# State space stage of a 512-token, three-block kernel: the turn before the norm's factor, tables by tile in HBM, fixed state buffers

## The chip, the cores and the metric

The kernel runs on one core of a Trainium2 chip. The metric is the device time of one execution in microseconds; before the change the median of 3 runs is 2787.21 us (2784.18 to 2787.91). Everything is in single precision. A product of two matrices is made of three matmuls: each operand is split into a high part (`Xh`, `whi`) and a low part (`Xl`, `wlo`), and high×high, low×high and high×low are added up.

## The reference, cut to what matters

512 tokens of 1024 channels pass through two layers and then a second block. The change touches the state space mixer of the second layer and the group norm of the retention in the second block:

```python
h = rms_norm(x, norm_mix[1])
y = s5_mixer(h, ...)                 # 64 groups of 16 channels, 64 complex states each
g_a, g_b = split(gelu(y) @ od_w_glu, 2)
x = x + g_a * sigmoid(g_b)

# s5_mixer: u -> B u -> x_t = a x_(t-1) + (B u)_t -> Re(C x) + d u
bu_re = einsum('gpc,bsgc->bsgp', bb_re, uf)      # and bu_im
_, _, xr, xi = associative_scan(combine, (a_r, a_i, bu_re, bu_im), axis=1)
y = einsum('gcp,bsgp->bsgc', c_re, xr) - einsum('gcp,bsgp->bsgc', c_im, xi) + d * uf

# retention, per head: r is 512 tokens x 256
r = (r - mean(r)) * rsqrt(var(r) + 1e-5) * gn_g
```

`rms_norm` multiplies each token by one factor, 1 / sqrt(mean of squares + eps), and each channel by its gain.

## The kernel before

The activations lie transposed: eight tiles `x[m]` of 128 channels by 512 tokens. All work is written in order per engine and the engines are ordered by semaphores; each engine runs its own instructions in program order, DMA issues included (SP issues most loads, ACT issues some DMAs). Weights come in tiles of 1 MB (`fetch`), and `cook` splits each into `whi` (ACT) and `wlo` (DVE or POOL, L342) one tile ahead of its use.

**Tables.** For the state space mixer, tables are made from its parameters while the first layer's feed-forward part runs (`s5_tables`, called step by step as `side` of `conv_ffn(0, ...)`): 16 steps, two for each tile of 128 channels; each step writes one block of 960 KB to HBM (`tabs[it]`, L1138). A block holds G (input into the turned states), C (states to output) and E (the rotations that turn the complex recurrence into a real one).

**The stage.** After the PLE part of layer one (`ple(0, ...)`, which adds up the squares of `x` tile by tile in `Rms.add`) the factor of the norm is made: sums over channels by matmul (L204), root on ACT (L177), three small DVE operations (L179 to L182), a diagonal matrix (`diag`, L190), a matmul that spreads it over the partitions (L197) and a copy `st_r` (L198). Then there are eight units, one for each tile of `x`. Per unit: `drive` makes `h` = x × gain × factor on DVE with the tokens taken in four phases (L1226) and writes it to HBM (`hd`, L1228); `lift` reads it back as `up`, with phases and channels turned into the partition axis (L1234); `load` reads the three tables (L1221). `mid` feeds: 16 matmuls of `up` with G (L1241), then six rotations with E on DVE (L1244 to L1249); `scan` runs the recurrence (two scans on DVE, L1260) and rotates back with E on POOL (L1267 to L1273; `xr` of odd units on DVE) into `xr` and `xi`, whose column zero is the state before the first token; `emit` makes 24 matmuls with C (L1281), GELU on ACT (`g`), a DMA out and `y` back (L1288); `land` splits `y` into `Gh` and `Gl`, which feed the GLU matmuls. A unit is fed at step t, scanned at t + 1, emitted at t + 2, landed at t + 3. The first half of the first GLU tile (`acc0[1]`) is multiplied between the units, the second half (`acc0[0]`) behind them.

**The retention.** `Head.retain` multiplies scores and values per head, takes mean and variance per token (BN_STATS and BN_AGGR on DVE), copies the variances to `gnv` (L1610), makes the factor with `rstd_of` (L174 to L182) and writes `rn` (L1613). `turn` transposes `rn` on PE (L1620) and scales it. The depthwise convolution's taps (L1519, DVE) are issued between the parts of a head, eight or sixteen at a time (`taps`).

## Time and profile before

| | us |
|---|---|
| median of 3 runs | 2787.21 |
| the profiled execution | 2786.97 |
| its span, first to last instruction | 2785.2 |
| TensorE (PE) busy | 2698.1 |
| VectorE (DVE) busy | 1581.5 |
| ScalarE (ACT) busy | 992.5 |
| GpSimd (POOL) busy | 666.9 |

The span leaves out what lies before the first and behind the last instruction, 1.8 us. Engines run beside each other, so their busy times overlap. The mean granted clock of TensorE is 0.987 of its full speed.

### The profile page before, as it was taken

What the parts mean: (1) busy time and instruction counts of PE and PEld (TensorE: products, weight loads), DVE (VectorE), ACT (ScalarE), POOL (GpSimd) and SP (SyncE); (2) the same over time, 40 slices, a digit from 0 to 9 for tenths busy, and PEclk for the clock granted to TensorE, in tenths of its full rate; (3) what the DMA queues carried; (4) which work ended last, traced back from release to release, by engine and by line L of the source; (5) the groups of instructions that cost most, each with busy time, mean ns of one, the idle gap of its engine ahead of it and who ended that gap; (6) DMA issues with size and microseconds to landing.
All of it is one profiled execution on the core that took longest, in us unless ns stands there. A gap on an engine that the chain in (4) does not pass through costs nothing. (4 is left out here: it accounts for less than half of the span.)

```text
span 2785.2 us, 35089 instructions
## 1 busy us (share of the span) xinstructions
PE 2698.1 (97%) x14355; PEld 2275.0 (82%) x14355; DVE 1581.5 (57%) x2478; ACT 992.5 (36%) x1295; POOL 666.9 (24%) x590
## 2 busy tenths in 40 slices
PE   8999999999579999999999999999999999999998
PEld 8978888887468888888888888887888788989888
DVE  5456968686654656466333335866387764733335
ACT  5544424344213423244212125333333352432222
POOL 2213035762351000002000026354443421300000
PEclk9999999999789999999999999999999999999999
DMA  5203334433762223224322232322222223222222
GB/s 162 76 31 107 99 105 148 148 132 133 224 207 91 91 91 101 96 76 136 101 96 91 92 105 82 95 82 81 97 81 97 76 91 109 89 91 91 91 95 72
DMA packets 277840, 289.80 MB, mean 104 GB/s; under 512 B 20197, under 2 KB 266951, under 8 KB 277680
## 3 DMA queue, kind: packets, MB, share of 16 engines
q1 hardware_dynamic: 256208, 260.38, 28.8%
q10 hardware_dynamic: 20640, 26.78, 2.7%
q8 instruction: 112, 1.84, 0.3%
q0 software_dynamic: 832, 0.41, 0.1%
q14 instruction: 48, 0.39, 0.0%
HBM read 263.43 MB, written 24.12 MB: 103 GB/s over the span
## 5 line engine op out<-in xcount | busy, mean ns | idle before, releaser
L339 ACT CAST whi<-raw 128x2048 fp32r<-128x2048 f32 (+2 forms) x216 | 406.3, 1881 | 761.4 <-PE ps L366 600.4
L365 PE MATMUL ps<-Xh,whi 128*128 128x512 f32 (+1 forms) x1472 | 567.4, 387 | 0.4 <-ACT Xh L302 0.4
L342 DVE TENSOR_TENSOR wlo<-raw,whi 128x2048 fp32r<-128x2048 f32 (+2 forms) x167 | 381.0, 2282 | 325.9 <-ACT whi L339 324.5
L366 PE MATMUL ps<-Xl,whi 128*128 128x512 f32 (+1 forms) x1472 | 563.0, 383 | 0.6 <-POOL Xl L305 0.6
L367 PE MATMUL ps<-Xh,wlo 128*128 128x512 f32 (+1 forms) x1472 | 562.7, 383 | 0.8 <-DVE wlo L342 0.8
L342 POOL TENSOR_TENSOR wlo<-raw,whi 128x2048 fp32r<-128x2048 f32 (+1 forms) x49 | 223.5, 4561 | 688.1 <-ACT whi L339 362.9
L365 PEld LDWEIGHTS ps<-Xh,whi 128*128 128x128 f32 x1472 | 276.2, 188 | 58.9 <-issue 3.2
L367 PEld LDWEIGHTS ps<-Xh,wlo 128*128 128x128 f32 x1472 | 276.7, 188 | 58.2 <-DVE wlo L342 1.6
L366 PEld LDWEIGHTS ps<-Xl,whi 128*128 128x128 f32 x1472 | 277.1, 188 | 56.9 <-issue 1.2
L365 PE MATMUL ps<-XBh,whi 128*128 128x512 f32 (+1 forms) x736 | 281.9, 385 | 1.0 <-ACT whi L339 1.0
L366 PE MATMUL ps<-XBl,whi 128*128 128x512 f32 (+1 forms) x736 | 281.0, 383 | 0.5 <-POOL XBl L305 0.5
L367 PE MATMUL ps<-XBh,wlo 128*128 128x512 f32 (+1 forms) x736 | 281.4, 384 | 0.0
L366 PE MATMUL ps<-Al,whi 128*128 128x512 f32 (+1 forms) x528 | 202.1, 383 | 1.5 <-DVE Al L305 1.5
L365 PE MATMUL ps<-Ah,whi 128*128 128x512 f32 (+1 forms) x528 | 202.6, 386 | 0.0
L367 PE MATMUL ps<-Ah,wlo 128*128 128x512 f32 (+1 forms) x528 | 202.5, 384 | 0.0
L1519 DVE SCALAR_TENSOR_TENSOR ps<-glu,par,ps 128x512 f32<-128x512 f32 x232 | 174.1, 751 | 4.1
L366 PEld LDWEIGHTS ps<-XBl,whi 128*128 128x128 f32 x736 | 138.2, 188 | 30.3 <-POOL XBl L305 0.9
L367 PEld LDWEIGHTS ps<-XBh,wlo 128*128 128x128 f32 x736 | 138.1, 188 | 29.9
L365 PEld LDWEIGHTS ps<-XBh,whi 128*128 128x128 f32 x736 | 137.6, 188 | 29.3 <-ACT whi L339 1.4
L222 POOL TENSOR_TENSOR st_a<-st_a,st_q 128x512 f32<-128x512 f32 x25 | 44.3, 1770 | 489.4 <-ACT st_q L220 489.3
L374 PE MATMUL ps<-whi,Xh 128*128 128x256 f32 (+1 forms) x512 | 147.6, 289 | 0.7 <-ACT z L608 0.4
L375 PE MATMUL ps<-wlo,Xh 128*128 128x256 f32 (+1 forms) x512 | 144.7, 283 | 0.0
(482 smaller groups left out, 4826.2 us busy)
## 6 DMA issues: line engine op xcount, KB each, us to landing
raw<-in_ffn_w_up_dram SPq DMA_DIRECT2D x66, 1024.0 KB, 5.1
raw<-in_w_in_dram SPq DMA_DIRECT2D x40, 1024.0 KB, 5.1
raw<-in_ffn_w_down_dram SPq DMA_DIRECT2D x32, 1024.0 KB, 4.8
raw<-in_ffn_w_gate_dram SPq DMA_DIRECT2D x22, 1024.0 KB, 5.2
tab<-tabs ACTq DMA_DIRECT2D x16, 960.0 KB, 3.9
raw<-in_ffn_w_down_dram SPq DMA_DIRECT2D x16, 768.0 KB, 4.1
raw<-in_ev_w_in_dram SPq DMA_DIRECT2D x8, 1024.0 KB, 5.2
raw<-in_ple_w_gate_dram SPq DMA_DIRECT2D x8, 1024.0 KB, 4.9
```

The source lines that it names most:

```text
L222: eng.tensor_tensor(self.acc, self.acc, sq, op=ALU.add)
L339: cp = act.copy(hi, rv)
L342: lo.tensor_tensor(lw, rv, hi.bitcast(F32), op=ALU.subtract)
L365: pe.matmul(acc, wh[j][:, s], X.h[k], start=start and t == 0, stop=False)
L366: pe.matmul(acc, wh[j][:, s], X.l[k], start=False, stop=False)
L367: pe.matmul(acc, wl[j][:, s], X.h[k], start=False, stop=stop and t == len(ks) - 1)
L374: pe.matmul(acc, X.h[k][:, s], wh[j], start=start and t == 0, stop=False)
L375: pe.matmul(acc, X.h[k][:, s], wl[j], start=False, stop=False)
L1519: vec.scalar_tensor_tensor(x[m] if t == 30 else acc, u[:, t:t + T], col("ck", t * KD + m), acc, op0=ALU.mult, op1=ALU.add)
```

## The change

- **Tables by tile.** A table block of HBM now holds one kind of table of one unit (4 phases), in rows of 4 KB or 6.5 KB: 48 DMAs write them instead of 16, and a unit loads with 3 DMAs on ACT's queue instead of 6 on SP's. Those of the first units are loaded during the PLE part.
- **Early turn.** `turn_in` makes `h` = x × gain on ACT, without the factor, as soon as PLE has done a tile, and `hd` and `up` follow at once.
- **The factor in turned order.** `rr` (each token's factor at its phase, 128 × 128, DVE) goes through one matmul with `l4` (L1345), which gives the factor in the order of the turned input; a copy `rbt`, and `norm` multiplies `up` by it: unit 0 on DVE, units 1 to 7 on POOL (L1250). `diag`, the spread matmuls and `st_r` go.
- **Fixed buffers.** Two pairs `xr`, `xi` and two `rm`, whose column zero is set once by six memsets. Back rotations of unit 7 run on DVE, the real part of units 0, 2, 4, 6 on POOL and of the odd ones on DVE.
- **Order of PE.** A unit is fed one step ahead; six eighths of `acc0[0]` are multiplied between the last units.
- **Elsewhere.** `Rms` uses two buffers for squares; a `warm` root on ACT is written ahead of tile 7's turn; POOL's weight split is cut into four operations; `retain` takes the variances without the copy, and the taps that followed or filled it are held behind the last `rn`.

```diff
--- before.py
+++ after.py
@@ cook @@
-            lo.tensor_tensor(lw, rv, hi.bitcast(F32), op=ALU.subtract)
+            q = kt * n // 4 if lo is pool else kt * n
+            for o in range(0, kt * n, q):
+                lo.tensor_tensor(lw[:, o:o + q], rv[:, o:o + q], hi[:, o:o + q].bitcast(F32), op=ALU.subtract)
@@ s5_tables @@
-            nc.scalar.dma_start(tabs[it], tab.rearrange("p q n -> p (q n)"))
+            i = it % 2
+            for z, (lo, hi) in CUT.items():
+                nc.scalar.dma_start(tabs[it // 2][z][:, 2 * i:2 * i + 2, :], tab[:, :, lo:hi])
@@ Unit @@
+            def table(self, tag, bufs):
+                lo, hi = CUT[tag]
+                t = ep.tile([P, 4, hi - lo], F32, tag=tag, name=nm(tag), bufs=bufs)
+                nc.scalar.dma_start(t, tabs[self.k][tag])
+                return t
...
+            def turn_in(self):
                 k = self.k
...
+                h = ep.tile([P, 4, P], F32, tag="h", name=nm("h"), bufs=2)
+                act.activation(h, x[k].rearrange("p (n j) -> p j n", j=4), AF.Copy, scale=col("norm_mix", KD + k))
+                nc.scalar.dma_start(hdr[k], h)
+                self.up = ep.tile([P, 4, P], F32, tag=f"Gh{k}", name=nm("up"))
+                src = hdr[k].rearrange("(i c) j n -> j c i n", c=32)
                 for b in range(4):
                     nc.sync.dma_start(self.up[32 * b:32 * b + 32], src[3 - b])
+            def norm(self, eng):
+                eng.tensor_tensor(self.up, self.up, rbt.unsqueeze(1).to_broadcast([P, 4, P]), op=ALU.mult)
@@ around ple @@
+        def ready(m):
+            rms2.add(m)
+            if m == KD - 1:
+                warm = sm.tile([P, 1], F32, tag="warm", name="warm")
+                act.activation(warm, eps_r, AF.Sqrt)
+            units[m].turn_in()
...
+        def phases():
+            b = bank((P, P))
+            pe.matmul(b, l4, rms2.rr.rearrange("p i n -> p (i n)"), start=True, stop=True)
+            vec.tensor_copy(rbt, b)
...
+        units[0].norm(vec)
+        units[0].feed()
+        units[2].load_g()
+        for k in range(1, KD):
+            units[k].norm(pool)
@@ the loop over units @@
+            if at(t + 1):
+                at(t + 1).feed()
+            if at(t + 3):
+                at(t + 3).load_g()
+            if at(t):
+                at(t).spin()
+                if at(t - 1) and t % 2 == 0:
+                    at(t - 1).real(vec)
...
+            if t == KD:
+                acc0[0] = [bank() for _ in range(2)]
+                mm_fm(acc0[1], w0s[1], G, [4], start=False, stop=False, js=[4])
+                for k in range(3):
+                    mm_fm(acc0[0], w0s[0], G, [k], start=k == 0, stop=False, js=[k])
@@ retain @@
-                vv = sm.tile([P, NT], F32, tag="gn_v", name=nm("gnv"))
-                vec.tensor_copy(vv, mv[:, :, 1])
-                r = rstd_of(vv, NT, LN_EPS)
+                r = rstd_of(mv[:, :, 1], NT, LN_EPS)
@@ the loop over heads @@
-                hd_.retain()
-                taps(8)
-            taps(16)
+                with tc.issue_after(hd_.retain().ins):
+                    taps(8 if j == 0 else 24)
```

Three places show how the change moves instructions. The first is DVE at the end of the PLE part, where the norm's factor (`rr`) is made; `st_a` holds the sum of squares. Before (six more rows L1226 follow, then the first rotation):

```order
L222 TENSOR_TENSOR st_a_6024<-st_a_6024,st_q_6447 128x512
L174 TENSOR_SCALAR ps_6516<-ps_6516 128x4
L179 RECIPROCAL rr_6523<-ps_6516 128x4
L180 SCALAR_TENSOR_TENSOR ps_6516<-ps_6516,rr_6523 128x4
L181 TENSOR_TENSOR ps_6516<-ps_6516,rr_6523 128x4
L182 SCALAR_TENSOR_TENSOR rr_6523<-ps_6516,rr_6523 128x4
L190 TENSOR_TENSOR diag_6528<-cst,rr_6523 128x512
L1226 SCALAR_TENSOR_TENSOR h_6567<-x_72,par,st_r_6550 128x512
L1226 SCALAR_TENSOR_TENSOR h_6570<-x_73,par,st_r_6550 128x512
```

After:

```order
L225 TENSOR_TENSOR st_a_6091<-st_a_6091,sq_6592 128x512
L174 TENSOR_SCALAR ps_6671<-ps_6671 128x4
L179 RECIPROCAL rr_6678<-ps_6671 128x4
L180 SCALAR_TENSOR_TENSOR ps_6671<-ps_6671,rr_6678 128x4
L181 TENSOR_TENSOR ps_6671<-ps_6671,rr_6678 128x4
L182 SCALAR_TENSOR_TENSOR rr_6678<-ps_6671,rr_6678 128x4
L1339 TENSOR_TENSOR rr<-s_6093,rr_6678 128x128
L1346 COPY rbt<-ps_6705 128x128
L1250 TENSOR_TENSOR up_6348<-up_6348,rbt 128x512
L1265 TENSOR_TENSOR s_896_6764<-tE_6371,ps_6725 128x512
L1266 TENSOR_TENSOR ps_6725<-tE_6371,ps_6725 128x512
```

The eight products `h` and the diagonal are gone from between the factor and the first rotation of unit 0 (the row that writes `s` from `tE` and `ps`, L1244, now L1265); a factor of 128 columns, a copy and one product take their place.

The second place is ACT ahead of the root of that factor (L177): squares of the last two tiles (`st_q`, `sq`), copies and DMAs of the PLE part (`Xl`, `pjd`). Before:

```order
L220 ACTIVATE st_q_6439<-x_78 128x512
L913 DMA pjd<-Xh_848_6476 128x512
L913 DMA pjd<-Xh_849_6477 128x512
L220 ACTIVATE st_q_6447<-x_79 128x512
L908 COPY Xl_852_6496<-ps_6498 128x512
L908 COPY Xl_853_6497<-ps_6499 128x512
L913 DMA pjd<-Xl_852_6496 128x512
L913 DMA pjd<-Xl_853_6497 128x512
L177 ACT_TABLE_LOAD
L177 ACTIVATE ps_6516<-ps_6516 128x4
```

After:

```order
L223 ACTIVATE sq_6592<-x_79 128x512
L1243 DMA hd_2561<-h_6579 128x512
L1242 ACTIVATE h_6597<-x_79,par 128x512
L921 DMA pjd<-Xh_870_6631 128x512
L1243 DMA hd_2562<-h_6597 128x512
L921 DMA pjd<-Xh_871_6632 128x512
L916 COPY Xl_874_6651<-ps_6653 128x512
L916 COPY Xl_875_6652<-ps_6654 128x512
L921 DMA pjd<-Xl_874_6651 128x512
L921 DMA pjd<-Xl_875_6652 128x512
L177 ACT_TABLE_LOAD
L177 ACTIVATE ps_6671<-ps_6671 128x4
```

The turned tiles `h` with their DMAs (L1242, L1243) now stand between the squares and the root, and the table load still stands just ahead of it.

The third place is DVE in the fourth retention head, from the variances (`mv`) to `rn`; L1519 (L1604 after) is a tap of the convolution. Before:

```order
L1610 COPY gnv_14708<-mv_14663 128x4
L1519 SCALAR_TENSOR_TENSOR ps_14654<-glu_14138,par,ps_14654 128x512
L174 TENSOR_SCALAR rv_14710<-gnv_14708 128x4
L1519 SCALAR_TENSOR_TENSOR ps_14654<-glu_14138,par,ps_14654 128x512 x3
L179 RECIPROCAL rr_14714<-rt_14712 128x4
L1519 SCALAR_TENSOR_TENSOR ps_14654<-glu_14138,par,ps_14654 128x512
L180 SCALAR_TENSOR_TENSOR rt_14712<-rv_14710,rr_14714 128x4
L1519 SCALAR_TENSOR_TENSOR ps_14654<-glu_14138,par,ps_14654 128x512
L181 TENSOR_TENSOR rt_14712<-rt_14712,rr_14714 128x4
L1519 SCALAR_TENSOR_TENSOR ps_14654<-glu_14138,par,ps_14654 128x512
L182 SCALAR_TENSOR_TENSOR rr_14714<-rt_14712,rr_14714 128x4
L1519 SCALAR_TENSOR_TENSOR ps_14654<-glu_14138,par,ps_14654 128x512
```

After:

```order
L1692 BN_AGGR mv_14738<-bs_14777 128x2
L1692 BN_AGGR mv_14738<-bs_14780 128x2
L174 TENSOR_SCALAR rv_14783<-mv_14738 128x4
L179 RECIPROCAL rr_14787<-rt_14785 128x4
L180 SCALAR_TENSOR_TENSOR rt_14785<-rv_14783,rr_14787 128x4
L181 TENSOR_TENSOR rt_14785<-rt_14785,rr_14787 128x4
L182 SCALAR_TENSOR_TENSOR rr_14787<-rt_14785,rr_14787 128x4
L1696 TENSOR_SCALAR rn_14737<-ps_14739,mv_14738,rr_14787 128x256 x2
L1696 TENSOR_SCALAR rn_14737<-ps_14755,mv_14738,rr_14787 128x256 x2
L1604 SCALAR_TENSOR_TENSOR ps_14729<-glu_14203,par,ps_14729 128x512 x4
L1706 SCALAR_TENSOR_TENSOR gnt_14872<-ps_14867,par,sg_14725 128x512
L1604 SCALAR_TENSOR_TENSOR ps_14729<-glu_14203,par,ps_14729 128x512
```

The copy `gnv` and eight taps that stood among the small operations are gone from there; `rn` follows the factor at once, and the taps come behind it.

## Rows read from the trace of the kernel before

**Rows 1.** The page: span, and busy time of each engine
```profile
span 2785.2 us, 35089 instructions
...
PE 2698.1 (97%) x14355; PEld 2275.0 (82%) x14355; DVE 1581.5 (57%) x2478; ACT 992.5 (36%) x1295; POOL 666.9 (24%) x590
```

**Rows 2.** Windows of the state space stage: PE, PEld, DVE, ACT, POOL busy (instructions), TensorE clock, DMA share, GB/s
```profile
720.00:740.00 20.00, 5.80 (x25) 5.56 (x26) 9.66 (x12) 0.00 (x0) 0.00 (x0) 0.50 0.87 285
740.00:800.00 60.00, 36.45 (x225) 33.88 (x224) 44.01 (x57) 11.53 (x16) 43.54 (x46) 0.71 0.74 221
...
840.00:860.00 20.00, 20.00 (x88) 16.23 (x87) 9.23 (x7) 5.63 (x8) 1.88 (x1) 1.00 0.34 106
700.00:840.00 140.00, 89.77 (x482) 77.01 (x481) 84.07 (x106) 32.80 (x48) 60.58 (x66) 0.78 0.68 210
```

**Rows 3.** Waits of PE from 700 to 840: total us, times, longest
```profile
PE ps L1241 <- DMA up<-hd: 19.5, 2, 13.4
PE ps L1241 <- DMA tG<-tab: 12.7, 3, 10.9
PE ps L365 <- ACT Gh L302: 10.6, 3, 6.0
```

**Rows 4.** Timeline of ACT from 708: start, duration, line, operation
```profile
708.40 0.63 ACT L220 ACTIVATE st_q<-x 128x512 f32<-128x512 f32 x1 [0.76 <-DVE st_a L222]
...
710.42 1.28 ACT L177 ACT_TABLE_LOAD   x1 [0.43 <-ACT Xl L908]
711.71 0.16 ACT L177 ACTIVATE ps<-ps 128x4 f32<-128x4 f32 x1
```

**Rows 5.** Timeline of DVE from 712 to 742
```profile
712.72 0.69 DVE L190 TENSOR_TENSOR diag<-cst,rr 128x512 f32<-128x512 f32 x1
...
736.99 0.68 DVE L1244 TENSOR_TENSOR s<-tE,ps 128x512 f32<-128x512 f32 x1
...
740.58 1.21 DVE L1260 TENSOR_TENSOR_SCAN zi<-s,ps 128x512 f32<-128x512 f32 x1
```

**Rows 6.** Timeline of PE, the last matmul of the last unit
```profile
824.76 0.39 PE L1281 MATMUL ps<-xi,tC 128*128 128x128 f32 x2
```

**Rows 7.** Timeline of POOL around 767
```profile
766.55 1.27 POOL L1269 TENSOR_TENSOR xr<-s,s 128x512 f32<-128x512 f32 x1
767.78 1.27 POOL L1273 TENSOR_TENSOR xi<-v,v 128x512 f32<-128x512 f32 x1
```

**Rows 8.** Timeline of DVE around 755
```profile
755.10 1.74 DVE L1269 TENSOR_TENSOR xr<-s,s 128x512 f32<-128x512 f32 x1 [2.72 <-POOL s L1267]
```

**Rows 9.** Timeline of ACT from 824
```profile
835.16 0.62 ACT L302 CAST Gh<-y 128x512 fp32r<-128x512 f32 x1 [8.23 <-DMA y<-hd]
```

**Rows 10.** Waits of PE from 1400 to the end
```profile
PE ps L1620 <- DVE rn L1613: 8.4, 4, 3.4
```

**Rows 11.** Timeline of DVE in one retention head
```profile
1905.62 0.17 DVE L1607 BATCH_NORM_AGGREGATE mv<-bs 128x2 f32<-128x6 f32 x1
...
1906.41 2.73 DVE L1610 COPY gnv<-mv 128x4 f32<-128x4 f32 x1
...
1915.24 1.90 DVE L1613 TENSOR_SCALAR rn<-ps,mv,rr 128x256 f32<-128x256 f32 x4
```

**Rows 12.** Timeline of POOL in the same head
```profile
1904.51 4.61 POOL L342 TENSOR_TENSOR wlo<-raw,whi 128x2048 fp32r<-128x2048 f32 x1 [6.61 <-ACT whi L339]
```

**Rows 13.** Timeline of PE in the same head
```profile
1915.93 0.41 PE L1620 MATMUL ps<-cst,rn 128*128 128x128 f32 x2 [3.35 <-DVE rn L1613]
```

**Rows 14.** Window around the other long wait of this kind, columns as in rows 2
```profile
2160.00:2180.00 20.00, 16.65 (x69) 13.51 (x68) 16.90 (x30) 2.37 (x4) 6.89 (x3) 0.83 0.16 53
```

**Rows 15.** DMA queues from 760 to 826: packets, MB, share of the window
```profile
q1 hardware_dynamic: 12564, 12.46, 63.8%
```

**Rows 16.** DMA queues from 380 to 640
```profile
q10 hardware_dynamic: 2160, 14.75, 13.7%
```

**Rows 17.** Window of the stage in which the tables are made
```profile
380.00:640.00 260.00, 257.74 (x1576) 207.67 (x1575) 199.19 (x357) 102.50 (x151) 155.93 (x242) 1.00 0.39 138
```

More of the change, by code (lines that the diff above doesn't have):

```diff
@@ L218, in add @@
             else:
-                sq = stile("st_q")
+                if self.two and self.n % 2:
+                    sq = xp.tile([P, T], F32, tag="diag", name=nm("sq"), bufs=2)
+                else:
+                    sq = stile("st_q")
                 act.activation(sq, x[m], AF.Square)
@@ L1199, in tile_net @@
             pass
-    rms2 = Rms()
-    rb2 = ple(0, X, rms, rms2.add, (rms2.fin1, rms2.fin2))
-    with tc.tile_pool(name="s5r", bufs=1) as rp:
+    with tc.tile_pool(name="s5e", bufs=1) as ep, ExitStack() as late:
+        rms2 = Rms(two=True)
         G = Act([None] * KD, [None] * KD)
@@ L1291, in land @@
                 k = self.k
-                G.h[k], G.l[k] = [rp.tile([P, T], F32R, tag=f"G{z}{k}", name=nm(f"G{z}")) for z in "hl"]
+                G.h[k] = ep.tile([P, T], F32R, tag=f"Gh{k}", name=nm("Gh"))
+                G.l[k] = rp.tile([P, T], F32R, tag=f"Gl{k}", name=nm("Gl"))
                 split(G.h[k], G.l[k], self.y.rearrange("p r n -> p (r n)"))
         units = [Unit(k) for k in range(KD)]
-        units[0].load()
-        for u in units:
-            u.drive()
-        units[0].lift()
@@ L1300, in tile_net @@
-        units[1].load()
-        for u in units[1:]:
-            u.lift()
+        def ready(m):
[4 more added lines that the diff above has]
+            units[m].turn_in()
+            if m == 1:
+                units[0].load_g()
+                units[0].load_e()
+            elif m == 3:
+                units[1].load_g()
+                units[1].load_e()
+            elif m == 5:
+                units[0].load_c()
+                units[2].load_e()
@@ new lines, in tile_net @@
+        s4 = ep.tile([P, 32], F32, name="s4")
+        vec.tensor_reduce(s4, ident.rearrange("p (n j) -> p n j", j=4), axis=AX.X, op=ALU.add)
+        m4 = ep.tile([P, 4], F32, name="m4")
+        vec.tensor_reduce(m4, ident.rearrange("p (n j) -> p j n", j=4), axis=AX.X, op=ALU.add)
+        l4 = ep.tile([P, P], F32, name="l4")
+        for b in range(4):
+            vec.tensor_copy(l4[:, 32 * b:32 * b + 32], m4[:, 3 - b:4 - b].to_broadcast([P, 32]))
+        ple(0, X, rms, ready, (chain, phases))
@@ new lines, in tile_net, with at @@
+        rp = late.enter_context(tc.tile_pool(name="s5r", bufs=1))
+        xrs = [[rp.tile([P, 4, P + 1], F32, name=f"x{z}{j}") for z in "ri"] for j in range(2)]
+        rms4 = [xt_(f"X{z}5") for z in "hl"]
+        for t in xrs[0] + xrs[1] + rms4:
+            pool.memset(t[:, :, 0:1], 0.0)
+        def at(k):
+            return units[k] if 0 <= k < KD else None
+        units[0].norm(vec)
[3 more added lines that the diff above has]
+            units[k].norm(pool)
@@ L1303, in tile_net @@
         acc0, w0s = {}, {}
+        for s in (1, 0):
+            w0s[s] = W(hold=s == 0)
         for t in range(KD + 4):
-            if t and t + 1 < KD:
-                units[t + 1].load()
-            if t < KD:
-                units[t].mid()
-            if 0 <= t - 1 < KD:
-                units[t - 1].scan()
+            if at(t + 1):
[6 more added lines that the diff above has]
+                    at(t - 1).real(vec)
@@ L1311, in tile_net @@
             if t == 2:
-                for s in (1, 0):
-                    w0s[s] = W(hold=s == 0)
                 acc0[1] = [bank() for _ in range(2)]
-            if 0 <= t - 3 < KD:
-                units[t - 3].land()
-            if 0 <= t - 2 < KD:
-                units[t - 2].emit()
-            if 0 <= t - 4 < KD:
-                k = t - 4
-                mm_fm(acc0[1], w0s[1], G, [k], start=k == 0, stop=k == KD - 1, js=[k])
+            if t > 1 and at(t + 1):
+                at(t + 1).load_e()
@@ L1322, in tile_net @@
+            if at(t - 4):
+                k = t - 4
+                if t != KD:
+                    mm_fm(acc0[1], w0s[1], G, [k], start=k == 0, stop=k == KD - 1, js=[k])
+                if t == KD + 1:
+                    for j in (3, 4, 5):
+                        mm_fm(acc0[0], w0s[0], G, [j], start=False, stop=False, js=[j])
+                elif t > KD + 1:
+                    mm_fm(acc0[0], w0s[0], G, [k], start=False, stop=k == KD - 1, js=[k])
             if t == KD:
@@ L1327, in tile_net @@
                 fetch(nxt[0] + 1)
-        acc0[0] = [bank() for _ in range(2)]
-        mm_fm(acc0[0], w0s[0], G, K8)
         X = new_x()
```

110 lines of the change are left out of this document (62 added, 48 removed).

## The prediction

> **What bounds the kernel now.** The page comes first: TensorE is busy for 2698.1 us of the span of 2785.2 [rows 1]. So 87 us of idle time, and what PE loses where its clock is low, is all that a change of this kind can win, and the question is which stretches hold it. The table of windows answers it [rows 2]. In the state space stage, from 700 to 840 us, PE works 89.77 of 140 us, so 50.2 us of the 87 lie here, and its granted clock is 0.78 in the mean. From 720 to 740 it works 5.80 us at 0.50, from 740 to 800 it works 36.45 of 60 us at 0.71; a clock of 0.50 is 1.2 GHz, the lower of its two levels. At 840 the stage is over: 88 matmuls fill 20.00 us, one every 0.227 us.
>
> The list of PE's waits in this stretch says for what it waits [rows 3]: 19.5 us for the turned input `up` (two waits, 13.4 us the longest), 12.7 us for the table `tG`, 10.6 us for `Gh`, the gated output that has come back from HBM. The first is a chain in series: root of the norm's factor on ACT at 711.71 [rows 4], the matrix `diag` on DVE at 712.72, a spread matmul, a copy, eight products, a DMA out and a DMA back, and only at 736.99 the first rotation (L1244) [rows 5]. From the root to the first rotation are 25.3 us. The last matmul of the last unit starts at 824.76 [rows 6].
>
> Behind the stage one more wait repeats: 8.4 us in four waits of PE for `rn` of a retention head [rows 10], of which the two long ones take 3.35 us [rows 13] and up to 3.4.
>
> **The start of the stage.** After the change the turned input doesn't need the factor, so the eight products and both DMAs of each tile are issued in the PLE stage, as each tile of `x` is done. What is left behind the root is: four small DVE operations (from the root 711.71 to `diag` 712.72, with the sequencing, 1.0 us), then `rr` with 128 columns, which I bound by the 4-column operation and by the 512-column `diag` of 0.69 us [rows 5] and take at 0.3; one matmul of 128 columns, a copy of 128 columns and their handovers, taken at 0.8 (between the 0.41 us of a 128-column pair of transposes [rows 13] and the 1.0 us of the small operations just counted); the product of unit 0 on DVE, 0.7 like `diag`; and eight feed matmuls of unit 0. Eight matmuls of 128 columns are 2 × 0.41 × 2 = 1.6 us by the transposes, about 1.5. Together 1.0 + 0.3 + 0.8 + 0.7 + 1.5 = 4.3 us.
>
> Against it, ACT carries more ahead of the root: `h` of tiles 6 and 7 and their two DMA issues stand between the squares and the table load (second order fence). One square takes 0.63 us [rows 4], so two more activations are 1.3; two DMA issues I estimate at half a square each, together 1.9 us, of which nothing may lie on the path if ACT waits there for PE anyway. The `warm` activation, which would take the table load of 1.28 us [rows 4] off this place, is at the head of ACT's program by the order, and a table load still stands in front of the root; I count nothing for it. First rotation: 711.7 + 1.9 + 4.3 = 717.9 against 736.99, so 19 us earlier.
>
> **The loop over eight units.** On DVE a unit has six rotations, one every 0.60 us (736.99 to 740.58 [rows 5]), and two scans of 1.2: 6.0 us, so 48 us for eight. To that come operations with both inputs in SBUF, which take from 0.69 like `diag` to 1.74 like `xr` beside a busy POOL [rows 5, 8]: the real parts of units 1, 3, 5 at 1.2 (3.6), the low parts of six returned tiles at 1.0 (6.0), since POOL is through with part of them, and six products of unit 7, which move from POOL to DVE when POOL has nothing left, at 0.7 (4.2). One split of a weight tile of four times 512 columns is 4 × 0.69 = 2.8. Sum 64.6, so DVE alone would end at 717.9 + 64.6 = 782.5.
>
> POOL has a pace of 1.23 us (766.55 to 767.78 [rows 7]). It now has seven products for the norm and, of units 0 to 6, six operations for the even ones and five for the odd: 7 + 24 + 15 = 46 operations, 56.6 us. It starts when the factor is there, near 715.7, and so ends near 772 without a wait, and near 777 if DVE holds it up five times by a microsecond. That is before DVE's end. Both engines are near their limit, so the sum goes by DVE: last product at 782.5, and with two microseconds for the last matmuls unit 7 ends at 784.5 instead of 824.76: 40.3 us. With the returned tiles and real parts in gaps, the bound below is 717.9 + 48 + 4.2 + 2 = 772; with a microsecond lost in each of the six to seven pairs that both engines share, the bound above is 791.
>
> **Behind the last unit.** `acc0[0]`, the second half of the first GLU tile, is partly done between the units. By the order 48 of its matmuls and `acc0[1]`'s are left behind the last unit's, before 63: 15 × 0.227 = 3.4 us. The round trip of the last tile takes from 824.9 to 835.16 + 0.62, so 10.9 us [rows 6, 9]; by the order 49 matmuls, the next weight tile's among them, stand ahead of the first that needs it: 49 × 0.227 = 11.1. So it is just hidden, and one late microsecond would show. I take 3.4, with 0 as the lower bound. Stage: 43.7 us.
>
> **The retention heads.** In the head of rows 11 the last statistics are there at 1905.62, then a 4-column COPY takes 2.73 us, since it stands beside a POOL subtraction that runs from 1904.51 to 1909.12 [rows 12], eight convolution taps stand among the operations that follow (third order fence), and `rn` is done at 1917.1 [rows 11]: 11.4 us. PE was through its cover at 1912.6 and waited 3.35 [rows 13]. The change drops the COPY, cuts the subtraction into four (4.61 / 4 = 1.15 us each), and holds back the taps. Then the first operation and the root, at most 1.0 like the small operations of the stage, those themselves 1.0, and 1.9 of `rn` are 3.9 us, and at most 1.2 more for one quarter: ready at 1909.5 to 1910.7, before PE is. All 8.4 us go. Around the other such wait the clock was 0.83 [rows 14]; of the 2.8 us that this costs of 16.65 busy ones I count half, because the transposes between run at either level. Term: 9.8, from 6 (some wait stays) to 11.2.
>
> The Trainium skill, SBUF — State Buffer, section "Who interferes with whom", says that a VectorE copy or tensor_scalar in its two-port mode and a GpSimd operation take one shared port pair, and that whoever comes second is blocked until the first is through. By that rule, which the end of the COPY at 1909.14 beside 1909.12 agrees with, the first small operation of the norm can inherit the stall, one quarter long; the sum is the same by the rule and by the rows, since PE's cover ends later than either.
>
> **What is costed at nothing.** The tables go to HBM in 48 DMAs instead of 16; 32 more issues on ACT in a stretch where ACT is busy for 102.50 of 260 us and PE for 257.74 at full clock [rows 17]. The cover is ACT's idle time and the weight tile that is split one ahead; without it each late tile costs what it is late. By the order, 96 DVE operations of the E tables run earlier in one bulk; DVE has 61 us free there [rows 17]. Memsets written once, another buffer for squares: the engines concerned idle there.
>
> **Sum.** 43.7 + 9.8 = 53.5 us from the profiled execution's 2786.97 (its span 2785.2 and 1.8 around it; the median, 2787.21, is 0.2 above): 2733.5, said as 2734. Its own range takes the loop from 772 to 791, the round trip and the retention term: 2720 to 2746.
>
> **Rivals.** *Transfers become the bound (0.17).* The stage is shorter and moves the same tables. A unit's G, E and C are 512 + 512 + 832 KB; two G, three E and two C come ahead, so 10.9 MB stay, with 4.2 MB of outputs both ways and 3 MB of weights: 18 MB in 66 us. The queue of loads moved 12.46 MB in 63.8% of 66 us, so 296 GB/s while busy [rows 15]; the queue that writes long rows moved 14.75 MB in 13.7% of 260 us, 414 GB/s [rows 16]. At 296 they fill 61 us of 66; with the tables at 414, 50. For it speaks that DMA's share is 0.74 now and 0.87 at the start [rows 2]; against it, rows of 4 KB in place of 1 KB. If the tables of six units come 2.5 us late each, the time is 2734 + 15 = 2749.
>
> The Trainium skill, DMA: Bandwidth & Descriptors, section "Issuing engines are not separate DMA queues", says that DMAs of different engines share the same 16 DMA engines and that issuing from more of them saves only sequencer time. By that, moving the tables from SP to ACT adds no rate, which is this rival; no row here has both arrangements side by side.
>
> *ACT's queue (0.10).* Table loads now stand between `rm`, GELU and casts on ACT, and each waits until its buffer is free, which POOL and PE decide. If every GELU waits 2 us so, in six of eight units, +12: 2746. For it: POOL is full, and E buffers come free from POOL's products. Against: the order has each load two units ahead of its use.
>
> *Only one part works (0.06).* Tile 7's turn goes out only just before the root, and by the round trip of 10.9 us it is back as late as 723; POOL reaches it after six others, 715.7 + 6 × 1.23 = 723. If lifts stand in SP's order behind one another and an early one is late too, the start wins 12 and not 19: 2741. Or `rn` still comes late: 2744.
>
> *More than I see (0.11).* The loop ends at its lower bound 772, 12.5 us earlier, and the retention gives 11.2: 2720; a higher clock for the matmuls of the stage gives the rest.
>
> *Slower or nothing (0.06).* The E bulk stands on DVE and ACT in front of the split of weights, in the stage where PE has no idle time and so nothing to give. The price is per weight tile: there are sixteen table steps, and the gain is used up when each makes PE wait 53.5 / 16 = 3.3 us. At 4.1 us each the time is 2734 + 66 = 2800. The 96 operations with 256 columns, at half of 0.69 each, are 33 us; in one piece they would cost that once, 2767, in pieces between weight tiles nothing. So slower has 0.04, no change 0.02.
>
> My forecast, the engines of the loop as the bound, keeps 0.50. The range reaches to the rivals on both sides, 2718 to 2755, and leaves out the last rival and the tails of the first. A difference under 0.2%, 5.6 us, can't be told from no change in this kernel. Faster 0.94, same 0.02, slower 0.04.
>
> **What the profile after would show.** Right: the first rotation near 718; PE's waits for `up` gone but for one of 4 to 6 us; POOL above 0.8 busy from 716 to 772; the last unit's matmuls near 785; no L1620-like wait for `rn`. Wrong: waits of PE or DVE for tE, tG, tC from DMA in most units (transfers); long waits of the GELU or `rm` behind DMA issues on ACT; PE below 257 of 260 us from 380 to 640 (the bulk of E).

## The result and the profile after

The changed kernel takes 2745.12 us, the median of 4 runs (2741.48 to 2747.23), against 2786.05 of the kernel before in as many; the ratio is 0.9852, with a 95% interval of 0.9835 to 0.9869. The profiled execution takes 2745.55 us and its span is 2743.8. That is 41 us less, inside the range and 11 us above the forecast of 2734, so every term has to be read by itself.

The two traces are best compared at events that both have. The sums of squares on PE (L204 in both) stand at the start of each part:

| L204 at | before | after | after minus before |
|---|---|---|---|
| end of the first feed-forward part | 652.93 | 657.46 | +4.5 |
| start of the state space stage | 709.81 | 714.69 | +4.9 |
| end of the stage and its GLU | 917.24 | 884.49 | −32.8 |
| start of the retention part | 1699.89 | 1665.82 | −34.1 |
| end of the retention part | 2223.50 | 2182.32 | −41.2 |

So the stage itself gave 37.6 us (207.43 before, 169.80 after), the retention part 7.1, the stretch between 1.3, and 4.9 were lost ahead of the stage. Of the stage's 37.6 us, 19.0 lie between the sum of squares and the first rotation, 15.7 between there and the last matmul of the last unit, and 3.0 behind it.

The windows of the changed kernel in the stage (columns as in [rows 2]):

```profile
720.00:740.00 20.00, 9.73 (x72) 8.79 (x73) 18.13 (x25) 3.80 (x3) 19.06 (x14) 0.93 0.60 201
740.00:760.00 20.00, 17.61 (x113) 16.68 (x113) 14.79 (x19) 3.94 (x7) 19.78 (x16) 0.82 0.66 224
760.00:780.00 20.00, 16.26 (x106) 14.08 (x105) 18.48 (x23) 3.46 (x6) 15.65 (x13) 0.91 0.80 256
780.00:800.00 20.00, 18.36 (x105) 15.44 (x104) 15.55 (x23) 6.25 (x11) 7.04 (x6) 1.00 0.61 192
800.00:820.00 20.00, 20.00 (x88) 16.11 (x87) 10.89 (x9) 10.16 (x12) 1.88 (x1) 1.00 0.27 84
```

From 720 to 740 PE was busy for 5.80 us before and is now for 9.73, and at 800 it is dense, 40 us sooner than before. The clock is 0.82 or more. The list of PE's waits in the changed kernel, 690 to 830 us (what waited for what, then total, times, longest):

```profile
PE ps L1303 <- POOL xr L1295: 7.9, 2, 6.5
PE ps L374 <- DVE Gl L311: 2.6, 3, 1.0
...
PE ps L1345 <- ACT st_s L916: 1.4, 1, 1.4
```

The waits for `up`, `tG` and most of those for `Gh` [rows 3] are gone; the largest is now the wait of the first emission for `xr`, which POOL makes. The timeline of DVE in the changed kernel shows the chain and the loop (start, duration, line, operation, in brackets the idle time before and what ended it):

```profile
718.86 0.18 DVE L179 RECIPROCAL rr<-ps 128x4 f32<-128x4 f32 x1 [2.91 <-ACT ps L177]
...
719.68 0.29 DVE L1339 TENSOR_TENSOR rr<-s,rr 128x128 f32<-128x128 f32 x1
...
720.90 0.69 DVE L1250 TENSOR_TENSOR up<-up,rbt 128x512 f32<-128x512 f32 x1
722.86 0.69 DVE L1265 TENSOR_TENSOR s<-tE,ps 128x512 f32<-128x512 f32 x1 [1.27 <-PE ps L1256]
...
743.26 1.74 DVE L1295 TENSOR_TENSOR xr<-s,s 128x512 f32<-128x512 f32 x1 [2.90 <-POOL s L1283]
...
754.16 0.69 DVE L1265 TENSOR_TENSOR s<-tE,ps 128x512 f32<-128x512 f32 x1 [1.11 <-DMA tE<-tE]
...
757.84 1.24 DVE L311 TENSOR_TENSOR Gl<-y,Gh 128x512 fp32r<-128x512 f32 x1 [1.19 <-ACT Gh L308]
...
790.57 0.69 DVE L1292 TENSOR_TENSOR xi<-s,s 128x512 f32<-128x512 f32 x1
```

The root stands at 718.67 (below), the first rotation at 722.86, and the last product of unit 7 ends at 791.26. In between DVE waits 2.90 us for POOL, 1.11 for a table `tE`, and 1.19 and more for `Gh`. The timeline of POOL from 716 to 740:

```profile
720.94 11.26 POOL L1250 TENSOR_TENSOR up<-up,rbt 128x512 f32<-128x512 f32 x7 [1.98 <-DMA up<-hd]
732.17 1.26 POOL L1284 TENSOR_TENSOR s<-tE,zi 128x512 f32<-128x512 f32 x1
```

Seven products for the norm take 11.26 us, and POOL comes to unit 0 only at 732.17. The timeline of PE at the last matmuls of the last unit:

```profile
794.96 0.39 PE L1303 MATMUL ps<-xi,tC 128*128 128x128 f32 x2
```

The timeline of ACT ahead of the root:

```profile
713.79 1.21 ACT L1242 ACTIVATE h<-x,par 128x512 f32<-128x512 f32 x1
...
717.38 1.28 ACT L177 ACT_TABLE_LOAD   x1 [0.41 <-ACT Xl L916]
718.67 0.16 ACT L177 ACTIVATE ps<-ps 128x4 f32<-128x4 f32 x1
```

The sum of squares is at 714.69, so the root follows it by 3.98 us. In the retention part, the list of PE's waits of the changed kernel from 1700 to 2240 us has no wait for `rn` [rows 10] any more, and two shorter ones stand there:

```profile
PE ps L374 <- POOL Rl L311: 1.3, 2, 0.6
PE ps L373 <- ACT Rh L308: 1.1, 1, 1.1
```

### The profile page after: what moved, and what is told of

It is laid out like the page before. It is cut to its first block, busy times and chain, and to the rows that moved or that the text cites. A ratio compares the mean times of both kernels' runs of the same rounds, so it can differ in the third digit from the quotient of the medians.

```text
span 2743.8 us, 35312 instructions
## 1 busy us (share of the span) xinstructions
PE 2692.1 (98%) x14355; PEld 2270.6 (83%) x14355; DVE 1562.4 (57%) x2475; ACT 999.5 (36%) x1302; POOL 684.0 (25%) x721
## 5 line engine op out<-in xcount | busy, mean ns | idle before, releaser
L350 POOL TENSOR_TENSOR wlo<-raw,whi 128x512 fp32r<-128x512 f32 (+1 forms) x196 | 248.4, 1299 | 664.8 <-ACT whi L345 340.1
L1604 DVE SCALAR_TENSOR_TENSOR ps<-glu,par,ps 128x512 f32<-128x512 f32 x232 | 170.4, 752 | 3.9
L225 POOL TENSOR_TENSOR st_a<-st_a,st_q 128x512 f32<-128x512 f32 x22 | 38.4, 1747 | 455.1 <-ACT st_q L223 455.0
```

Source lines behind the costliest of these rows:

```text
L225: eng.tensor_tensor(self.acc, self.acc, sq, op=ALU.add)
L350: lo.tensor_tensor(lw[:, o:o + q], rv[:, o:o + q], hi[:, o:o + q].bitcast(F32), op=ALU.subtract)
L1604: vec.scalar_tensor_tensor(x[m] if t == 30 else acc, u[:, t:t + T], col("ck", t * KD + m), acc, op0=ALU.mult, op1=ALU.add)
```

## The experiments

Times are medians in us, and ratios are to the kernel before, measured beside each group of runs on the same chip: 2787.62 for runs 1, 2, 3 and 5, 2787.27 for 6, 7, 8 and 11, 2788.42 for 4, 9, 10 and 12. Stretches are read from one traced execution of each kernel; executions of the changed kernel lie up to 5.8 us apart, so a stage that is 1 or 2 us longer or shorter is weak evidence. "Stage" is the time between the two sums of squares that enclose the stage, 169.80 in the changed kernel.

**1. The table writes split, alone (b_split).** On the kernel before:

```diff
-            nc.scalar.dma_start(tabs[it], tab.rearrange("p q n -> p (q n)"))
+            for lo, hi in ((0, 256), (704, 960), (256, 704)):
+                nc.scalar.dma_start(tabs[it].rearrange("p (q n) -> p q n", q=2)[:, :, lo:hi], tab[:, :, lo:hi])
```

> The kernel before, with each table step writing its block in three DMAs (G, E, C) to the same rows of HBM; loads are unchanged. Theory A (the bulk of E operations delays the feed-forward part): with its own DMA the E part of a buffer comes free early, the E operations move up in the order as in the changed kernel, PE waits about 3.8 us once behind a late DVE operation of the convolution near 418 us, and the sum of squares behind the feed-forward part (653 us before) comes 2 to 5 us later; time +2 to +5 us. Rival B (the 4.5 us of lag come from another part of the change, such as the quartered weight split or the squares' two buffers): no lag there, time within 1 us of before.

2789.85 against 2787.62, ratio 1.001 (1.000 to 1.002). The sum of squares at 652.93 came at 656.46. The window of this kernel from 380 to 640 us:

```profile
380.00:640.00 260.00, 254.54 (x1560) 204.49 (x1559) 188.60 (x343) 99.64 (x146) 150.98 (x242) 1.00 0.40 136
```

PE loses 5.5 us of 260 where it lost 2.3 before [rows 17]. The lag of 3.5 us is there with this edit alone: theory A, though with waits of 2.1 us twice and not 3.8 once. It is the trace that shows it: the median is 2.2 us higher, and its interval reaches down to no change.

**2. E's DMA held behind C's (a_epin).** On the changed kernel:

```diff
-            for z, (lo, hi) in CUT.items():
-                nc.scalar.dma_start(tabs[it // 2][z][:, 2 * i:2 * i + 2, :], tab[:, :, lo:hi])
+            for z in ("tG", "tC"):
+                lo, hi = CUT[z]
+                end = nc.scalar.dma_start(tabs[it // 2][z][:, 2 * i:2 * i + 2, :], tab[:, :, lo:hi])
+            lo, hi = CUT["tE"]
+            with tc.issue_after(end.ins):
+                nc.scalar.dma_start(tabs[it // 2]["tE"][:, 2 * i:2 * i + 2, :], tab[:, :, lo:hi])
```

> The changed kernel, with the DMA of E held behind that of C in each table step, so that the E operations spread again over the steps as before. Theory A (the bulk costs the lag): the wait of 3.8 us goes, the sum of squares behind the feed-forward part falls from 657.5 back to 653 to 654.5, time -2 to -4.5 us against the changed kernel. Rival B: no change, within 1 us of the changed kernel.

2739.77 (ratio to before 0.9827, 0.9812 to 0.9842). The stage starts at 709.36 in place of 714.69, and takes 169.53. The window of this kernel from 380 to 640 us:

```profile
380.00:640.00 260.00, 260.00 (x1586) 209.55 (x1585) 197.98 (x360) 103.45 (x154) 155.54 (x243) 1.00 0.41 139
```

PE has no idle time left there; in the changed kernel's window it has 4.1 us:

```profile
380.00:640.00 260.00, 255.92 (x1559) 205.97 (x1558) 188.63 (x343) 100.22 (x146) 146.36 (x241) 0.99 0.40 134
```

Theory A holds, and the loss is 5.3 us. Its place is ACT's queue, in the timeline of ACT of the changed kernel:

```profile
386.47 11.08 ACTq L1150 DMA_DIRECT2D tE<-tabs  x4
397.64 1.91 ACT L345 CAST whi<-raw 128x2048 fp32r<-128x2048 f32 x1 [11.99 <-DVE s5o L1188]
...
409.58 1.92 ACT L345 CAST whi<-raw 128x2048 fp32r<-128x2048 f32 x1 [3.88 <-DVE tabs L1190]
```

ACT stands for 11.08 us at four DMA issues of `tE`, each of which waits for E operations on DVE, and the next cast of a weight tile (`whi`) comes after 11.99 us of idle time. The cast after that waits behind two more such issues and starts at 409.58. In the kernel of this run, with E pinned, it starts 8.7 us earlier, by its timeline of ACT:

```profile
400.88 1.90 ACT L345 CAST whi<-raw 128x2048 fp32r<-128x2048 f32 x1 [3.56 <-PE ps L374]
```

In the changed kernel's timeline of PE the lateness ends in this wait:

```profile
418.02 1.96 PE L1137 MATMUL ps<-tabs,abd 128*32 128x32 f32 x32 [3.77 <-DVE cv L864]
```

In the changed kernel's windows around it the granted clock falls too, where it is 1.00 in this run's kernel and in the kernel before, so the wait costs more than its 3.77 us:

```profile
410.00:420.00 10.00, 6.23 (x54) 4.91 (x52) 9.77 (x20) 4.79 (x8) 1.87 (x5) 0.81 0.51 169
420.00:430.00 10.00, 10.00 (x37) 7.95 (x38) 9.90 (x18) 4.90 (x7) 9.24 (x14) 0.85 0.28 94
```

**3. The retention part alone (b_ret).** On the kernel before, POOL's weight split in one piece:

```diff
-                vv = sm.tile([P, NT], F32, tag="gn_v", name=nm("gnv"))
-                vec.tensor_copy(vv, mv[:, :, 1])
-                r = rstd_of(vv, NT, LN_EPS)
+                r = rstd_of(mv[:, :, 1], NT, LN_EPS)
...
-                hd_.retain()
-                taps(8)
-            taps(16)
+                with tc.issue_after(hd_.retain().ins):
+                    taps(8 if j == 0 else 24)
```

> The kernel before, with the retention part of the change alone: variances read without the copy, taps held behind rn; POOL's weight split stays in one piece. Theory A (taps and copy made rn late): the waits for rn fall from 8.4 us to under 1 us, time -6 to -9 us. Rival B (POOL's long operation beside the first small operation was the cause): the first small operation takes 2 to 3 us in the copy's place, one to two waits of 1 us or more stay; time -3 to -6 us.

2787.75 against 2787.62, ratio 0.9999 (0.9989 to 1.0008): nothing won. Yet no wait for `rn` is left in the trace, and the retention part is 8.4 us shorter. What was lost lies elsewhere: from 1385 to 1585, where no instruction differs, PE is busy all the time at full clock, but the window of this kernel shows fewer matmuls:

```profile
1385.00:1585.00 200.00, 200.00 (x859) 160.94 (x858) 66.35 (x56) 45.48 (x40) 0.00 (x0) 1.00 0.29 93
```

859 matmuls stand in 200 us, where the kernel before has 867. The start of one to that of the next is 233.3 ns there, 231.1 before. And the first small operation did inherit the stall, in this kernel's timelines of DVE and of POOL:

```profile
1909.24 3.86 DVE L174 TENSOR_SCALAR rv<-mv 128x4 f32<-128x4 f32 x1
```

```profile
1908.45 4.62 POOL L342 TENSOR_TENSOR wlo<-raw,whi 128x2048 fp32r<-128x2048 f32 x1 [2.31 <-ACT whi L339]
```

The 4-column operation ends at 1913.10, POOL's at 1913.07.

**4. The same with the small tile left allocated (b_retpad).**

```diff
+                vv = sm.tile([P, NT], F32, tag="gn_v", name=nm("gnv"))
+                pool.memset(vv, 0.0)
                 r = rstd_of(mv[:, :, 1], NT, LN_EPS)
```

> The retention part of the change alone on the kernel before, as in the run named b_ret, but the small tile that held the copied variances stays allocated (POOL sets it to zero), so that every later tile of that pool lies where it lay before. Theory A (the part saves the 8.4 us that its trace shows, and the loss elsewhere, 512-column matmuls every 233 ns instead of 231, came with the place of the tiles): matmuls are back at 231 ns and the time is 7 to 9 us under the kernel before. Rival B (the slow matmuls come with the order of the instructions, or the gain is not there): 233 ns again, or time within 3 us of the kernel before.

2778.36 against 2788.42, ratio 0.9964 (0.9951 to 0.9977), and in the same window of this kernel the matmuls are back at 867 in 200 us:

```profile
1385.00:1585.00 200.00, 200.00 (x867) 162.62 (x866) 66.38 (x56) 45.46 (x40) 0.00 (x0) 1.00 0.30 95
```

So theory A by its numbers; that the place of the tiles is the cause is inferred (last section). The retention part takes 516.4 us (523.6 before): 7.2 of the 10 us lie there.

**5. POOL's weight split in four, alone (b_quart).** On the kernel before:

```diff
-            lo.tensor_tensor(lw, rv, hi.bitcast(F32), op=ALU.subtract)
+            q = kt * n // 4 if lo is pool else kt * n
+            for o in range(0, kt * n, q):
+                lo.tensor_tensor(lw[:, o:o + q], rv[:, o:o + q], hi[:, o:o + q].bitcast(F32), op=ALU.subtract)
```

> The kernel before, with POOL's weight split in four operations and nothing else. Theory A (taps and copy): the copy falls from 2.7 to at most 1.2 us, the two long waits for rn shrink by about 1.5 us each, time -2 to -4 us. Rival B (POOL's long operation): both long waits go, -6 to -8 us. If the lag ahead of the stage comes from the four operations: the sum of squares at 653 us comes 2 us or more later.

2777.97 against 2787.62, ratio 0.9964 (0.9951 to 0.9976). The retention part takes 517.7 us, 6.0 less; the state space stage is 3.3 shorter too, and why is open (in runs 1, 3 and 4, which don't touch its instructions, it takes 206.5 to 208.8 us). The copy in the head of [rows 11], in this kernel's timeline of DVE:

```profile
1901.12 0.66 DVE L1612 COPY gnv<-mv 128x4 f32<-128x4 f32 x1
...
1908.35 0.99 DVE L1615 TENSOR_SCALAR rn<-ps,mv,rr 128x256 f32<-128x256 f32 x2
```

The copy takes 0.66 us in place of 2.73; two waits for `rn`, 3.5 us in all, are left of 8.4. In the waits it lies between the two expectations, and the whole time fell by more than either, 9.7 us. The long POOL operation made more of the lateness than theory A gives it, the copy and the taps together the rest; those two weren't tried apart.

**6. Norms of units 1 to 3 on DVE (a_norm4).**

```diff
+        for k in range(1, 4):
+            units[k].norm(vec)
...
-        for k in range(1, KD):
+        for k in range(4, KD):
             units[k].norm(pool)
```

> The changed kernel, with the norm's product of units 1 to 3 on DVE as well, so that POOL has four of them and not seven. Theory A (the loop's end hangs on POOL, which reaches the products of unit 0 only at 732.2 us, 4.6 after DVE could give them): POOL's first product comes near 728, DVE's wait of 2.9 us for POOL and PE's wait of 6.5 us for xr shrink by 3 us or more, the last product of unit 7 comes 3 to 4 us earlier and the time falls by as much against the changed kernel. Rival B (DVE or transfers hold the loop): DVE has 2.1 us more to do, the last product comes 0 to 2 us later.

2740.54 (ratio 0.9833, 0.9819 to 0.9846). The time is lower, but not where this edit acts: the stage takes 171.16, 1.4 longer, while 2.5 us less are lost ahead of it and the retention part takes 3.0 less, where no instruction differs. The granted clock does (last section). The timelines of DVE and of POOL:

```profile
718.45 5.73 DVE L1250 TENSOR_TENSOR up<-up,rbt 128x512 f32<-128x512 f32 x4
...
728.82 2.26 DVE L350 TENSOR_TENSOR wlo<-raw,whi 128x2048 fp32r<-128x2048 f32 x1
```

```profile
718.49 6.81 POOL L1250 TENSOR_TENSOR up<-up,rbt 128x512 f32<-128x512 f32 x4 [2.08 <-DMA up<-hd]
728.97 3.23 POOL L1284 TENSOR_TENSOR s<-tE,zi 128x512 f32<-128x512 f32 x1 [3.67 <-DVE zi L1277]
```

Four products that DVE does in 0.7 each take 5.73 while POOL does its own, and POOL's first product of unit 0 takes 3.23 beside DVE's weight split of 2.26. The two engines took turns: moving the work won nothing, and the last product came 1.4 us later behind the sum of squares. Rival B.

**7. Half of the C tables (a_halfc).** It leaves out half of C: two of four phases are loaded and used twice.

```diff
-                nc.scalar.dma_start(t, tabs[self.k][tag])
+                n = 2 if tag == "tC" else 4
+                nc.scalar.dma_start(t[:, 0:n], tabs[self.k][tag][:, 0:n])
...
-                        pe.matmul(py[:, i, :], self.C[:, i, c:c + P], rhs, start=st == 0, stop=st == 2)
+                        pe.matmul(py[:, i, :], self.C[:, i % 2, c:c + P], rhs, start=st == 0, stop=st == 2)
```

> The changed kernel, which loads only half of each unit's C table (two of four phases, used twice), so that 3.4 MB of 10.9 MB of table loads are left out; the output is not the reference's. Theory A (engines hold the loop): the last product of unit 7 moves by less than 1.5 us, time within 2 us of the changed kernel. Rival B (transfers): the DMA of the gated output takes 5 us instead of 7 to land, the waits of DVE for Gh (0.5 to 1.2 us, four times) and for tE (1.1 us) go, last product 3 to 5 us earlier and the time with it.

2741.49 (ratio 0.9834, 0.9821 to 0.9848). The stage takes 166.39, 3.4 less, and the last product starts 1.3 us earlier behind the sum of squares. The table of DMA issues from 716 to 780 us, KB each and median us to landing, of the changed kernel:

```profile
tC<-tC ACTq DMA_DIRECT2D x5, 832.0 KB, 7.3
...
hd<-g ACTq DMA_DIRECT2D x5, 256.0 KB, 7.0
```

and with half of C:

```profile
tC<-tC ACTq DMA_DIRECT2D x6, 416.0 KB, 4.1
hd<-g ACTq DMA_DIRECT2D x5, 256.0 KB, 4.4
```

The gated output lands in 4.4 us and not in 7.0, and no wait for `tE` is left. Rival B in its mechanism: half of C's transfers cost the stage 3.4 us. Not in its place: the last product moved by 1.3 us only, inside theory A's bound, and the rest came between it and the last matmul (1.2) and behind that (0.9).

**8. The early root behind the last sigmoid (a_warm).**

```diff
-                act.activation(warm, eps_r, AF.Sqrt)
+                with tc.issue_after(sig[0].ins):
+                    act.activation(warm, eps_r, AF.Sqrt)
```

> The changed kernel, with the early root on ACT held behind the last sigmoid, so that the table load stands there and not in front of the root of the norm. Theory A (ACT's queue is on the path to the factor): the root comes 1.0 to 1.4 us earlier behind the last matmul for its sum, and the time falls by 1 to 1.4 us, which the trace can show and the clock hardly. Rival B (POOL's wait for the turned input of tile 1 to 7, 2.0 us before its first norm, takes its place): the first rotation comes earlier, the last product doesn't, time unchanged.

2748.10 (ratio 0.9858, 0.9845 to 0.9872), stage 172.06, 2.3 longer. The timeline of ACT in this kernel: the table load moved, but the root came 6.1 us behind the sum of squares, 4.0 in the changed kernel:

```profile
709.30 1.28 ACT L1326 ACT_TABLE_LOAD   x1
...
717.71 1.08 ACT L917 COPY Xl<-ps 128x512 f32<-128x512 f32 x2 [0.40 <-ACT Xh L917]
720.77 0.81 ACTq L922 DMA_DIRECT2D pjd<-Xl  x2
721.63 0.16 ACT L177 ACTIVATE ps<-ps 128x4 f32<-128x4 f32 x1 [2.85 <-DMA up<-hd]
```

The load pushed copies behind the turned tiles, and the root then stood behind their DMA issues, which ended at 721.6. Neither expectation: ACT's queue is on the path, but by what stands in it, not by the table load.

**9. Late split of a weight tile (a_wlate).** The call that cooks the second GLU tile moves from ahead of the loop to its step 3:

```diff
-        for s in (1, 0):
-            w0s[s] = W(hold=s == 0)
         for t in range(KD + 4):
+            if t == 3:
+                for s in (1, 0):
+                    w0s[s] = W(hold=s == 0)
```

> The changed kernel, with the split of the second GLU weight tile cooked at the fourth step of the loop and not ahead of it, so that this DVE operation of 2.3 us no longer stands between the two scans of unit 0. Theory A (operations with two inputs in SBUF on DVE and POOL exclude each other, and this one holds up both at the start): the second scan of unit 0 comes 2.2 us earlier, DVE does the split where it waited 2.9 us for POOL, the last product comes 1.5 to 3 us earlier behind the sum of squares. Rival B (transfers set the pace): the last product moves by less than 1 us.

2744.14 (ratio 0.9841, 0.9826 to 0.9856), stage 169.68. The split left the start, and the last product came 1.1 us earlier behind the sum of squares, between the two expectations; the stage is as long as in the changed kernel.

**10. The root two groups earlier (a_fin).**

```diff
-                ahead_of_time(w, 4, "Xl6", "Xl7")
                 fins[0]()
+                ahead_of_time(w, 4, "Xl6", "Xl7")
```

> The changed kernel, with the sums for the norm's factor and its root written two projection matmul groups earlier, so that on ACT the table load follows the last turned tile at once, ahead of two copies and their DMA issues. Theory A (ACT's queue is on the path): root 2.0 to 2.5 us earlier behind the last square, last product 1 to 2.5 us earlier, time -1 to -2.5 us. Rival B: the earlier matmuls make PE wait 2.5 us longer for the sum, and nothing is won: time within 1 us.

2747.64 (ratio 0.9848, 0.9831 to 0.9866), stage 174.90, 5.1 longer. The root came 1.6 us earlier behind the sum of squares and all of it was lost behind. The timeline of DVE in this kernel:

```profile
718.07 0.29 DVE L1339 TENSOR_TENSOR rr<-s,rr 128x128 f32<-128x128 f32 x1
724.78 0.29 DVE L1346 COPY rbt<-ps 128x128 f32<-128x128 f32 x1 [6.42 <-PE ps L1345]
```

The factor was ready at 718.36, but its matmul stands on PE behind 24 projection matmuls that now follow the sum, and DVE waited 6.42 us for it. Rival B, and worse: the path went through PE's order. PE waited 3.64 us for the sum (0.78 in the changed kernel), and behind that wait the granted clock fell, so half of the 24 matmuls came one every 0.43 us; in this kernel's window:

```profile
715.00:722.00 7.00, 7.00 (x21) 5.78 (x22) 1.15 (x6) 2.27 (x4) 0.00 (x0) 0.53 0.61 196
```

**11 and 12. Edits together.** Edits 2, 6 and 8 (a_all):

> The changed kernel with three edits together: E's DMA held behind C's, the norms of units 1 to 3 on DVE, the early root behind the last sigmoid. If the effects add: -5 of the first, -3 of the second, -1 of the third, 2735 to 2738 us in place of 2745 of the changed kernel. If the loop is held by transfers: only the first counts, 2740.

2742.91 (ratio 0.9837, 0.9824 to 0.9850): the stage starts at 709.53, as with edit 2, and takes 174.58. Edits 2, 9 and 10 (a_best):

> The changed kernel with three edits: E's DMA held behind C's, the late split and the earlier root. If they add: -5, -2 and -1.5 us, so 2736 to 2738 us in place of 2745. If only the first counts: 2740.

2741.24 (ratio 0.9828, 0.9814 to 0.9843): start at 709.48, stage 173.87. In both the first edit brings its 5 us, and the others take most of it back in the trace (the stage is 5.1 and 4.3 us longer than with edit 2 alone) and 3.1 and 1.5 us of it in the medians. Edit 2 alone has the lowest median of all that ran. It beats the kernel before by far more than its interval; against the changed kernel (0.9852, 0.9835 to 0.9869) the intervals overlap, so there only the trace shows its 5.3 us, at the place where it acts.

## Why the prediction was right, and where it was off

**The start.** From the root to the first rotation 4.3 us were predicted; 718.67 to 722.86 are 4.2; the first rotation, forecast for 717.9, comes 4.9 later, which is what was lost ahead of the stage. ACT's additional work was put at 1.9 us; the root stands 3.98 us behind the sum of squares, 1.90 before, so 2.1. The first term held in each of its parts, and so did the reading that `warm` does nothing. The second is right by luck: two activations were taken at 0.63 us each, but one of `h` takes 1.21, and only tile 7's stands behind the last square.

**What was costed at nothing** failed first. The bulk of E was seen in the order, and its cover was said to be ACT's idle time and the weight tile split one ahead. The 6 chances in 100 for slower or nothing went to a price that uses up the whole gain; a small price had none. It was 4.9 us here, 3.5 in run 1 and 5.3 in run 2, and the sign that the prediction named for it, PE below 257 of 260 us, is there with 255.92. The free time of DVE was not the point. ACT's queue, which ran in order, stood at DMA issues which waited for DVE (11.08 us at four of them), and the casts of weights stood behind these.

**The loop.** The sum of DVE's work was 64.6 us; 68.4 passed between the first rotation and the last product. DVE worked for some 61.7 of them and waited 6.7 (2.9 for POOL, 2.7 for `Gh`, 1.1 for `tE`). So the work was a little over-counted and the waits were left out. Run 7 leaves out half of C and has a stage 3.4 us shorter: the rival "transfers become the bound" was true to a part of its 15 us. Run 6 shows that POOL's lateness couldn't be bought off with DVE's time, since their products, with both inputs in SBUF, took turns. From the last product to the last matmul 2 us were taken, and it took 3.7, as PE still had four GLU matmuls, a wait of 0.6 us for `Gl` and twenty of the unit's own matmuls to do. From the first rotation to the last matmul the prediction has 21.2 us less than before; 15.7 were measured. How these divide among tables by tile, the work moved between DVE and POOL and PE's order is open, as no run takes the stage's parts apart. That the early turn gave the 19.0 us ahead of the first rotation is read from the rows alone: the eight products and their DMAs are gone from that path.

**Behind the last unit.** From the last matmul of the last unit to the end of the part 92.5 us passed before and 89.5 after: 3.0, where 3.4 were predicted.

**The retention heads.** 9.8 us were predicted and 7.1 measured. The waits for `rn` went, all 8.4 us, but waits for `Rl` and `Rh` rose from 0.2 to 2.4 us: what was late next, and left out. The term for the clock came out by where a fall lies: before, the granted clock was low around the last wait for `rn` [rows 14]; after, it is 1.00 there, but low at the start of the part, for reasons that no run shows. Runs 2 and 6, with the same waits and no such fall in the part, take 513.5 us, 10.1 less than before. So the traced 7.1 is near the low end, and 9.8 is less wrong than it looks. The cause was half right. Held-back taps without the copy (run 4, −7.2 in this part) and the cut of POOL's operation (run 5, −6.0) each win nearly all of it, and both together 7.1: either one brings `rn` ahead of PE, and the second has little left to win. That the first small operation can inherit the stall, which the prediction took from the Trainium skill's page SBUF — State Buffer, section "Who interferes with whom", is what run 3 has in full: 3.86 us, ending 0.03 us behind POOL's operation.

**The sum.** In order: +4.9 where 0 was said, −37.6 where −43.7, −1.3 where 0, −7.1 where −9.8. The misses, 4.9 + 6.1 − 1.3 + 2.7 = 12.4, are the 12.1 us between the 2733.5 of the sum and the 2745.55 of the profiled execution, but for 0.2 gained behind the last of these events and the rounding.

## What to carry to other kernels

When a buffer comes free earlier, a scheduler fills it with the work that waited for it; look which in-order queue will then stand behind that work's DMA, and pin the DMA where the work used to be. An operation of a few columns on a path can be held up for as long as a long operation of POOL beside it runs (3.86 us in run 3), so cut the long neighbour. Before a step is moved forward on one engine, follow the result through the next engine's order: of four attempts to shorten this stage (runs 6, 8, 9 and 10) three have a longer one in the trace, by 1.4, 2.3 and 5.1 us, and one is as long as before.

## What the runs showed of the hardware

The pace of dense matmuls at full granted clock was not the same in all programs: 231.1 ns from one 512-column matmul to the next in the kernel before, 233.3 ns in run 3, and 231 again in run 4, which differs by one tile of four numbers per partition and its memset. Over the program this hid a gain of 8 us. The changed kernel, which has no such tile either, has 231.1 too, so it isn't the missing tile by itself. That the place of the tiles in SBUF is the cause is inferred; the memset wasn't tried apart from it.

Stretches in which no instruction differs don't last equally long in all versions. In those that leave E's DMA free, the sum of squares ahead of the stage came at 712.1 to 715.5 us, and at 709.4 to 709.5 in the three that pin it. The retention part took 516.5 us in the changed kernel and 513.5 in run 6, with the same waits of PE for `Rl` and `Rh` (2.4 us). The difference is the granted clock at its start, in the windows of the changed kernel and of run 6:

```profile
1665.00:1672.00 7.00, 6.41 (x31) 6.21 (x31) 3.28 (x12) 0.60 (x3) 0.49 (x1) 0.54 0.00 0
```

```profile
1664.00:1671.00 7.00, 6.42 (x49) 5.94 (x50) 3.69 (x14) 0.36 (x3) 0.25 (x1) 1.00 0.00 0
```

PE is busy for as long in both, but finishes 31 matmuls in one and 49 in the other. In the 5 us ahead (from 1660.5 and from 1659.26) PE had worked for 3.45 us in both, so what decides whether the clock falls isn't shown. Of a total that moves by 3 us, the part that an edit did is read from the stretch where it acts, and the granted clock of that stretch with it.
